# Attention probabilities scaled on ScalarE, the gate's Silu tied to a transpose copy, S5 products tied behind the mixing products

## The chip, the cores and the metric

The kernel runs on one core of a Trainium2 chip. The metric is the time of one execution on the device in microseconds (us). The engines are named as in the profile: PE is TensorE (matrix products and transposes), PEld its weight loads, DVE VectorE, ACT ScalarE, POOL GpSimd, SP SyncE, which issues most of the DMA transfers. PE's clock has two levels, 2.4 and 1.2 GHz; the profile's granted clock is 1.00 where the higher one was granted throughout.

## The reference

A decoder trunk of two layers over 1024 positions and 1024 channels, in float32. The change lies in the first layer's mixer, which has two groups of heads:

```
def rms_norm(x, g): y = x * rsqrt(mean(x * x) + EPS); return y * g
hn = rms_norm(x, norm_ab[i])
z = hn @ w_in_ab[i]
q, k, v, g_a, v_b, g_b = jnp.split(z, [...])           # 1024 columns each
a_out = dilated_attention(q, k, v) * jax.nn.silu(g_a)  # 16 heads of 64
b_out = multiscale_pool(v_b, pool_w[i], pool_scale[i]) * jax.nn.silu(g_b)
y = jnp.concatenate([a_out, b_out], axis=-1) @ w_out_ab[i]
```

`dilated_attention` mixes three causal patterns, (window, dilation) = (128, 1), (512, 4) and (2048, 16), by their softmax denominators, which is the same as one softmax over all keys of the three. In short: `p = exp(sc - m); o = (p / den) @ v`, with `den` the sum of a row of `p`.

The second layer has a gated spatial unit and an S5 state-space layer (complex diagonal states, 32 groups), whose tables depend on the parameters alone. After each mixer stands a cross-attention into 256 memory tokens.

## The kernel before

Large products are made in three passes (`mm3`, lines 199 to 207): weights and activations are split into a high part and a rest, and PE does high by high, high by rest, rest by high. The weights come through one planned queue: SP loads a tile of 128x1024 (`wst`), ACT rounds it to its high part (L177, `wh`), DVE subtracts (L178, `wl`).

The stage of the change is the input projection of the first layer, with the attention inside it. Two generators run against each other in `drive`: `ab_main` makes the projections, for each of 8 pairs of heads V (every second pair), then q, k and the gate `ga` (`ab_pair`, 24 products of 128x512 for each half of the sequence); after them the pooling group (`ab_pool`). `ab_side` does the attention. Each `yield 1` of `ab_main` (twice per 24 products) adds `rate` to an account, and at 1.0 one step of `ab_side` is written, so that a burst of attention stands after every 1 / `rate` yields. `yield 0` of the side means that it had nothing to do; `yield 2` of the main means that it waits for the side, and the next step is written at once.

One step of `ab_side` is one **burst**, for block b of 128 queries of a pair (8 blocks a pair, 64 in all):

- `turn` of the block before: PE transposes its probabilities `P` for two heads (L547, L551; PSUM tiles `ps_t`, two buffers), ACT copies the first part of each head to `PT` (L553), DVE copies the rest to `PTr` (L556).
- `front` of block b: PE's scores (L519, `ps_s`), then per head DVE's addition of the mask (L526) and maximum (L527), ACT's Exp with the row sum `den` (L528), DVE's reciprocal (L529) and multiplication of `P` by it (L530). A block has from 160 columns (b = 0) to 512 (b = 7).
- `mix` of the block before: PE's products of `PT` with V (L566, `ps_o`); after blocks 3 and 7 `last` (L577) adds the far keys and DVE multiplies by the gate (L580).

PE's instructions of this stage keep the written order (`in_order`); those of the other engines are placed by a scheduler, in which the side has the higher priority. Beside the bursts `behind` issues one step of `s5_prep`, the S5 tables, mostly small operations on POOL, some transposes and products on PE (L1125, L1131) and one reciprocal on DVE (L1028). These are `loose`: not held in PE's written order, but tied behind three instructions of the burst, `s.anchors`: the last score product, the last maximum and the last Exp.

In `ab_pair` the gate's Silu (L497) is issued when the second half of `ga` is evicted, and only then is the pair handed to the attention.

Of the kernel before, what the change touches and what calls it, by code (L numbers as in the profile page):

```python
# [95 lines left out]
class Prog:  # L96
# [372 lines left out]
    def ab_pair(s, pr):  # L469
        nc = s.nc  # L470
        q, kk, ga = (s.b(n) for n in ("q", "kk", "ga"))
        V, Vp = s.b("V"), s.b("Vp")
        vd, c0 = s.vd[pr // 2], 128 * (pr % 2)
        for r in range(4):
            nc.sync.dma_start(V[32 * r:32 * r + 32, :].rearrange("i (t c) -> i t c", t=8),
                              vd[:, c0:c0 + 128].rearrange("(t i r) c -> r i t c", i=32, r=4)[r])
        for hh in range(2):
            nc.sync.dma_start(Vp[:, 512 * hh:512 * hh + 512].rearrange("p (r c) -> p r c", r=4),
                                vd[512 * hh:512 * hh + 512, c0:c0 + 128].rearrange("(p r) c -> p r c", r=4))
        held, R8 = {}, s.R8  # L480
        for h in range(2):
            yield from s.proj(("ab", pr), h, held)
            s.anchor = nc.vector.tensor_tensor(q[:, 512 * h:512 * h + 512].rearrange("p (b r i) -> p b r i", b=4, r=4),
                                               s.last.rearrange("p (b i r) -> p b r i", b=4, r=4),
                                               R8[h].rearrange("p (b i r) -> p b r i", b=4, r=4), op=ALU.mult)
            yield 1
        for h in range(2):
            yield from s.proj(("ab", 8 + pr), h, held)
            s.anchor = nc.vector.tensor_tensor(kk[:, 512 * h:512 * h + 512].rearrange("p (b r i) -> p b r i", b=4, r=4),
                                               s.last.rearrange("p (b i r) -> p b r i", b=4, r=4),  # L490
                                               s.R[h].rearrange("p (b i r) -> p b r i", b=4, r=4), op=ALU.mult)
            yield 1
        for h in range(2):
            yield from s.proj(("ab", 16 + pr), h, held)
            s.anchor = nc.vector.tensor_tensor(ga[:, 512 * h:512 * h + 512], s.last, s.R[h], op=ALU.mult)
            if h == 1:
                nc.scalar.activation(ga, ga, AF.Silu)  # L497
            yield 1
        s.pair[pr] = (q, kk, ga, V, Vp)

    def attn(s, pr):

# [4 lines left out]
        def front(b):  # L507
# [15 lines left out]
            for e in range(2):  # L523
                t = s.u("P")
                mx, den = s.col("mx"), s.col("den")
                nc.vector.tensor_tensor(t[:, :n], p[e][:, :n], s.cst[:, m0:m0 + n], op=ALU.add)  # L526
                i = nc.vector.tensor_reduce(mx, t[:, :n], axis=AX.X, op=ALU.max, negate=True)  # L527
                j = nc.scalar.activation(t[:, :n], t[:, :n], AF.Exp, bias=mx, accum_out=den)  # L528
                nc.vector.reciprocal(den, den)  # L529
                nc.vector.tensor_scalar(t[:, :n], t[:, :n], den, None, op0=ALU.mult)  # L530
                P[b, e] = t
            s.anchors += [i, j]

        def turn(b):
# [8 lines left out]
            for e in range(2):  # L543
# [6 lines left out]
                    c0 = 128 * (nb + k)  # L550
                    nc.tensor.transpose(pt[:, c0:c0 + 128], t[:, 128 * k:128 * k + 128], s.ident)  # L551
                PT[b, e] = s.u("PT")
                nc.scalar.activation(PT[b, e][:, :n1], pt[:, :n1], AF.Copy)  # L553
                for k in range(kt):
                    w, c0 = min(128, n2 - 128 * k), 128 * (nb + k)
                    nc.vector.tensor_copy(PTr[half, e][:w, 512 * k:512 * k + 512].rearrange("p (r b i) -> p r b i", r=4, b=4)[:, :, b4, :],  # L556
                                          pt[:w, c0:c0 + 128].rearrange("p (r i) -> p r i", r=4))

        def mix(b):
            half, b4 = b // 4, b % 4  # L560
            nb = 1 if b == 0 else 2
            for j in range(nb):
                blk = b - nb + 1 + j
                for e in range(2):
                    ov = o[half][64 * e:64 * e + 64, :].rearrange("p (r b i) -> p r b i", r=4, b=4)[:, :, b4, :]
                    nc.tensor.matmul(ov, lhsT=V[:, 128 * blk + 64 * e:128 * blk + 64 * e + 64],  # L566
                                     rhs=PT[b, e][:, 128 * j:128 * j + 128].rearrange("p (r i) -> p r i", r=4),
                                     start=(b4 == 0 and j == 0), stop=False, skip_group_check=True)

# [25 lines left out]
    def ab_side(s):  # L595
# [3 lines left out]
        for n in range(64 + 2):  # L599
            pr, b = divmod(n, 8)  # L600
            if n < 64:
                while pr not in s.pair:
                    yield 0
                if b == 0:
                    made[pr] = s.attn(pr)
            was, wb = divmod(n - 1, 8)
            if 0 < n <= 64:
                made[was][1](wb)
            if n < 64:
# [38 lines left out]
    def ab_main(s):  # L648
        s.R8 = [s.u("R8") for _ in range(2)]
        for h in range(2):  # L650
            s.nc.gpsimd.tensor_scalar(s.R8[h], s.R[h], 0.125, None, op0=ALU.mult)
        s.vd, s.pair, s.gd, s.attn_done = {}, {}, {}, -1
        for pr in range(8):
            if pr % 2 == 0:
                yield from s.ab_v(pr // 2)
# [830 lines left out]
def build(nc, tc, a):  # L1486
    with tc.tile_pool(name="sb", bufs=1) as pool, tc.tile_pool(name="ps", bufs=1, space=MS.PSUM) as psum, \
# [11 lines left out]
        s.phase = "ab"  # L1499
        s.mtags = ("mm",)  # L1500
        mark = len(nc.cur_bb.bb.instructions)
        drive(tc, s.ab_main(), s.ab_side(), 0.55, -500)
        pe = [i for i in nc.cur_bb.bb.instructions[mark:] if i.engine == s.anchors[0].ins.engine]
        s.in_order(pe[0], pe[-1])
        s.mtags = wide
# [27 lines left out]
```

## Time and profile before

| | |
|---|---|
| time, median of 3 runs | 2112.68 us (2112.36 to 2113.53) |
| the profiled execution | 2116.89 us, span 2115.2 us |
| granted clock, mean over the span | 0.989 |
| PE busy | 2061.8 us (97%) |
| DVE busy | 1144.8 us (54%) |
| ACT busy | 767.5 us (36%) |
| POOL busy | 534.8 us (25%) |

The span is the time from the first to the last instruction on the core. Busy time counts what an engine executes, not its waits. The attention bursts lie between about 260 and 835 us of the span.

### The profile page before, as it was taken

To read this page: it belongs to the slowest core of one execution; us is meant where nothing else is said; L and a number is where in the kernel's file an instruction comes from. 1 tells how busy PE (TensorE), PEld (TensorE's weight loads), DVE (VectorE), ACT (ScalarE), POOL (GpSimd) and SP (SyncE) were. 2 spreads that over 40 slices of the span, in tenths; PEclk is the share of its full clock that TensorE was granted. 3 is DMA by queue.
4 is the path that set the end of the run, shared out by engine and by line. 5 is a ranking of instruction groups with operands and counts; after the bars stand their busy time and mean duration, and the time that the engine had idled before them with its cause. 6 is when DMAs were issued, how large, how long until landed. Compare 5 with 4: busy or idle time off the path is not lost.

```text
span 2115.2 us, 33157 instructions
## 1 busy us (share of the span) xinstructions
PE 2061.8 (97%) x12974; PEld 1729.7 (82%) x12974; DVE 1144.8 (54%) x2067; ACT 767.5 (36%) x1442; POOL 534.8 (25%) x802
## 2 busy tenths in 40 slices
PE   8999999899999988999999999999999999999998
PEld 8999888687787766888888888888888887888887
DVE  6664266566655775456453655444653334555554
ACT  7765243333333333114332444212221122443453
POOL 4332017722333244122111003221221100220013
PEclk9999999999999999999999999999999999999999
DMA  7888212103114112116464125532331134642142
GB/s 293 301 292 281 73 33 86 56 24 119 51 65 114 62 51 86 56 66 222 146 208 164 46 101 183 166 119 70 116 113 70 58 102 157 202 165 74 51 169 80
DMA packets 131468, 258.63 MB, mean 122 GB/s; under 512 B 13040, under 2 KB 63344, under 8 KB 131312
## 3 DMA queue, kind: packets, MB, share of 16 engines
q1 hardware_dynamic: 86608, 189.39, 26.8%
q0 software_dynamic: 13440, 43.53, 5.6%
q10 hardware_dynamic: 31264, 23.60, 3.6%
q8 instruction: 102, 1.67, 0.3%
q14 instruction: 54, 0.44, 0.1%
HBM read 193.02 MB, written 63.44 MB: 121 GB/s over the span
## 4 chain that ended last, share of the span: by engine, by line
PE 87%; DVE 5%; POOL 3%; ACT 2%; issue 2%; DMA 1%; SPq 0%; DVEq 0%; ACTq 0%; POOLq 0%
PE ps_mm L203 13%; PE ps_mm L204 13%; PE ps_mm L205 13%; PE ps_s L204 5%; PE ps_s L205 5%; PE ps_s L203 5%; PE ps_o L205 4%; PE ps_o L204 4%; PE ps_o L203 4%; PE ps_s L519 2%; PE ps_o L566 1%; PE ps_mm L1311 1%; PE ps_mm L1309 1%; PE ps_mm L1310 1%; PE ps_t L547 1%
## 5 line engine op out<-in xcount | busy, mean ns | idle before, releaser
L178 DVE TENSOR_TENSOR wl<-wst,wh 128x1024 fp32r<-128x1024 f32 (+1 forms) x263 | 345.8, 1329 | 128.3 <-ACT wh L177 123.3
L203 PE MATMUL ps_mm<-xg,wh 128*128 128x512 f32 x880 | 350.1, 398 | 1.3 <-DVE ug L1338 1.0
L204 PE MATMUL ps_mm<-xg,wh 128*128 128x512 f32 x880 | 343.7, 391 | 0.0
L205 PE MATMUL ps_mm<-xg,wl 128*128 128x512 f32 x880 | 343.3, 390 | 0.0
L177 ACT ACTIVATE wh<-wst 128x1024 fp32r<-128x1024 f32 (+1 forms) x263 | 262.0, 1016 | 113.4 <-PE ps_mm L204 84.5
L203 PEld LDWEIGHTS ps_mm<-xg,wh 128*128 128x128 f32 x880 | 165.4, 188 | 43.3 <-issue 8.3
L205 PEld LDWEIGHTS ps_mm<-xg,wl 128*128 128x128 f32 x880 | 165.3, 188 | 34.9
L204 PEld LDWEIGHTS ps_mm<-xg,wh 128*128 128x128 f32 x880 | 165.6, 188 | 32.4 <-issue 0.2
L240 POOL TENSOR_TENSOR acc<-acc,sq 128x512 f32<-128x512 f32 (+1 forms) x81 | 102.5, 1266 | 215.0 <-ACT sq L236 202.5
L223 ACT ACTIVATE xg<-x,gains 128x512 fp32r<-128x512 f32 x64 | 46.2, 722 | 246.3 <-DVE x L753 187.4
L528 ACT ACTIVATE P<-P,mx 128x320 f32<-128x320 f32 (+7 forms) x128 | 77.9, 610 | 136.6 <-DVE mx L527 132.9
L553 ACT ACTIVATE PT<-ps_t 128x256 f32<-128x256 f32 (+1 forms) x128 | 45.3, 369 | 174.2 <-PE ps_t L551 172.7
L592 POOL DMA_DIRECT2D gab<-G x32 | 18.1, 567 | 244.2 <-DVE G L580 126.9
L530 DVE TENSOR_SCALAR P<-P,den 128x320 f32<-128x320 f32 (+7 forms) x128 | 77.2, 604 | 4.4
L556 DVE COPY PTr<-ps_t 128x128 f32<-128x128 f32 (+2 forms) x192 | 46.0, 281 | 55.8 <-ACT PT L553 52.8
L224 DVE SCALAR_TENSOR_TENSOR xg<-x,gains,xg 128x512 fp32r<-128x512 f32 x64 | 52.1, 815 | 42.1 <-ACT xg L223 40.8
L203 PE MATMUL ps_mm<-wh,xg 128*128 128x256 f32 x256 | 73.9, 289 | 0.0
L205 PE MATMUL ps_mm<-wh,xg 128*128 128x256 f32 x256 | 72.5, 283 | 0.0
L204 PE MATMUL ps_mm<-wl,xg 128*128 128x256 f32 x256 | 72.4, 283 | 0.0
L1338 DVE TENSOR_TENSOR ug<-ps_mm,R 128x512 f32<-128x512 f32 x32 | 22.1, 689 | 90.4 <-PE ps_mm L205 90.3
L526 DVE TENSOR_TENSOR P<-ps_s,cst 128x320 f32<-128x320 f32 (+7 forms) x128 | 65.0, 549 | 8.3 <-PE ps_s L519 6.4
L547 PE MATMUL ps_t<-cst,P 128*128 128x128 f32 x240 | 47.5, 281 | 21.0 <-DVE den L529 15.0
(423 smaller groups left out, 5115.1 us busy)
## 6 DMA issues: line engine op xcount, KB each, us to landing
wst<-w_ab SPq DMA_DIRECT2D x40, 512.0 KB, 3.4
wst<-w_out_ab SPq DMA_DIRECT2D x32, 512.0 KB, 4.3
wst<-vsc SPq DMA_DIRECT2D x32, 512.0 KB, 4.0
wst<-w_kv SPq DMA_DIRECT2D x31, 512.0 KB, 5.9
wst<-w_cd SPq DMA_DIRECT2D x24, 512.0 KB, 3.4
wst<-w_out_cd SPq DMA_DIRECT2D x32, 384.0 KB, 3.3
wst<-w_q SPq DMA_DIRECT2D x16, 512.0 KB, 8.1
msc<-mo ACTq DMA_DIRECT2D x32, 256.0 KB, 6.2
```

What stands on the lines that cost most here:

```text
L177: s.last_hi = s.nc.scalar.activation(H[:, :w], t[:, :w], AF.Copy)
L178: s.nc.vector.tensor_tensor(L[:, :w], t[:, :w], H[:, :w], op=ALU.subtract)
L203: s.nc.tensor.matmul(ps, lhsT=lh, rhs=rh, start=(i == 0), stop=False)
L204: s.nc.tensor.matmul(ps, lhsT=lh, rhs=rl, start=False, stop=False)
L205: s.nc.tensor.matmul(ps, lhsT=ll, rhs=rh, start=False, stop=(i == n - 1))
L223: nc.scalar.activation(H, x, AF.Copy, scale=g)
L224: nc.vector.scalar_tensor_tensor(L, x, g, H, op0=ALU.mult, op1=ALU.subtract)
L240: nc.gpsimd.tensor_tensor(st["acc"][:, :n], st["acc"][:, :n], q[:, :n], op=ALU.add)
L526: nc.vector.tensor_tensor(t[:, :n], p[e][:, :n], s.cst[:, m0:m0 + n], op=ALU.add)
L528: j = nc.scalar.activation(t[:, :n], t[:, :n], AF.Exp, bias=mx, accum_out=den)
L530: nc.vector.tensor_scalar(t[:, :n], t[:, :n], den, None, op0=ALU.mult)
L547: nc.tensor.transpose(pt[:, 128 * j:128 * j + 128], t[:, n2 + 128 * j:n2 + 128 * j + 128], s.ident)
```

## The change

The multiplication of the probabilities by `1/den` goes from a DVE `tensor_scalar` to an ACT Copy with a per-row scale. A pair is handed to the attention before its gate is projected; the Silu of the gate is issued in the burst that turns block 2, tied behind the second PT copy, and `ab_side` waits there until the gate is projected. The first of the three anchors of the S5 steps is the last mixing product in place of the last score product. The rate of bursts goes from 0.55 to 0.52.

```diff
--- before.py
+++ after.py
@@ -490,13 +490,13 @@
                                                s.last.rearrange("p (b i r) -> p b r i", b=4, r=4),
                                                s.R[h].rearrange("p (b i r) -> p b r i", b=4, r=4), op=ALU.mult)
             yield 1
+        s.pair[pr] = (q, kk, ga, V, Vp)
         for h in range(2):
             yield from s.proj(("ab", 16 + pr), h, held)
             s.anchor = nc.vector.tensor_tensor(ga[:, 512 * h:512 * h + 512], s.last, s.R[h], op=ALU.mult)
             if h == 1:
-                nc.scalar.activation(ga, ga, AF.Silu)
+                s.gated.add(pr)
             yield 1
-        s.pair[pr] = (q, kk, ga, V, Vp)
 
     def attn(s, pr):
 
@@ -527,7 +527,7 @@
                 i = nc.vector.tensor_reduce(mx, t[:, :n], axis=AX.X, op=ALU.max, negate=True)
                 j = nc.scalar.activation(t[:, :n], t[:, :n], AF.Exp, bias=mx, accum_out=den)
                 nc.vector.reciprocal(den, den)
-                nc.vector.tensor_scalar(t[:, :n], t[:, :n], den, None, op0=ALU.mult)
+                nc.scalar.activation(t[:, :n], t[:, :n], AF.Copy, scale=den)
                 P[b, e] = t
             s.anchors += [i, j]
 
@@ -550,11 +550,14 @@
                     c0 = 128 * (nb + k)
                     nc.tensor.transpose(pt[:, c0:c0 + 128], t[:, 128 * k:128 * k + 128], s.ident)
                 PT[b, e] = s.u("PT")
-                nc.scalar.activation(PT[b, e][:, :n1], pt[:, :n1], AF.Copy)
+                i = nc.scalar.activation(PT[b, e][:, :n1], pt[:, :n1], AF.Copy)
                 for k in range(kt):
                     w, c0 = min(128, n2 - 128 * k), 128 * (nb + k)
                     nc.vector.tensor_copy(PTr[half, e][:w, 512 * k:512 * k + 512].rearrange("p (r b i) -> p r b i", r=4, b=4)[:, :, b4, :],
                                           pt[:w, c0:c0 + 128].rearrange("p (r i) -> p r i", r=4))
+            if b == 2:
+                with s.tc.issue_after(i.ins):
+                    nc.scalar.activation(ga, ga, AF.Silu)
 
         def mix(b):
             half, b4 = b // 4, b % 4
@@ -563,7 +566,7 @@
                 blk = b - nb + 1 + j
                 for e in range(2):
                     ov = o[half][64 * e:64 * e + 64, :].rearrange("p (r b i) -> p r b i", r=4, b=4)[:, :, b4, :]
-                    nc.tensor.matmul(ov, lhsT=V[:, 128 * blk + 64 * e:128 * blk + 64 * e + 64],
+                    s.anchors[0] = nc.tensor.matmul(ov, lhsT=V[:, 128 * blk + 64 * e:128 * blk + 64 * e + 64],
                                      rhs=PT[b, e][:, 128 * j:128 * j + 128].rearrange("p (r i) -> p r i", r=4),
                                      start=(b4 == 0 and j == 0), stop=False, skip_group_check=True)
 
@@ -604,6 +607,8 @@
                 if b == 0:
                     made[pr] = s.attn(pr)
             was, wb = divmod(n - 1, 8)
+            while wb == 2 and was not in s.gated:
+                yield 0
             if 0 < n <= 64:
                 made[was][1](wb)
             if n < 64:
@@ -649,7 +654,7 @@
         s.R8 = [s.u("R8") for _ in range(2)]
         for h in range(2):
             s.nc.gpsimd.tensor_scalar(s.R8[h], s.R[h], 0.125, None, op0=ALU.mult)
-        s.vd, s.pair, s.gd, s.attn_done = {}, {}, {}, -1
+        s.vd, s.pair, s.gated, s.gd, s.attn_done = {}, {}, set(), {}, -1
         for pr in range(8):
             if pr % 2 == 0:
                 yield from s.ab_v(pr // 2)
@@ -1499,7 +1504,7 @@
         s.phase = "ab"
         s.mtags = ("mm",)
         mark = len(nc.cur_bb.bb.instructions)
-        drive(tc, s.ab_main(), s.ab_side(), 0.55, -500)
+        drive(tc, s.ab_main(), s.ab_side(), 0.52, -500)
         pe = [i for i in nc.cur_bb.bb.instructions[mark:] if i.engine == s.anchors[0].ins.engine]
         s.in_order(pe[0], pe[-1])
         s.mtags = wide
```

What this does to the order of the instructions, at three places. First PE, where the third pair begins (block 0 of the pair; the bursts that turn block 7 of the pair before and then block 0). Before:

```order
L519 MATMUL ps_s<-kk,q 32x128 x8
L519 MATMUL ps_s<-kk,q 32x32 x8
L566 MATMUL ps_o<-PT,V 64x4x32 x4
L547 MATMUL ps_t<-cst,P 128x128
L551 MATMUL ps_t<-cst,P 128x128
L547 MATMUL ps_t<-cst,P 128x128
L551 MATMUL ps_t<-cst,P 128x128
L519 MATMUL ps_s<-kk,q 32x256 x8
L519 MATMUL ps_s<-kk,q 32x64 x8
L566 MATMUL ps_o<-PT,V 64x4x32 x2
```

After the change:

```order
L519 MATMUL ps_s<-kk,q 32x128 x8
L519 MATMUL ps_s<-kk,q 32x32 x8
L569 MATMUL ps_o<-PT,V 64x4x32 x4
L203 MATMUL ps_mm<-xg_648,wh 128x512
L204 MATMUL ps_mm<-xg_648,wh 128x512
L205 MATMUL ps_mm<-xg_648,wl 128x512
...
L547 MATMUL ps_t<-cst,P 128x128
L551 MATMUL ps_t<-cst,P 128x128
```

The mixing products (L566, now L569) were followed at once by the transposes of the next burst; now 24 products of the projection stand between (8 times the three rows shown).

ACT, at the gate of the third pair (`ga`); L528 is Exp, L553 the copy of transposed probabilities. Before:

```order
L528 ACTIVATE P,den<-P,mx 128x512 x2
L553 ACTIVATE PT<-ps_t 128x256
L497 ACT_TABLE_LOAD
L497 ACTIVATE ga<-ga 128x1024
L553 ACTIVATE PT<-ps_t 128x256
L528 ACT_TABLE_LOAD
L528 ACTIVATE P,den<-P,mx 128x160 x2
L553 ACTIVATE PT<-ps_t 128x128 x2
```

After the change:

```order
L553 ACTIVATE PT<-ps_t 128x256 x2
L560 ACT_TABLE_LOAD
L560 ACTIVATE ga<-ga 128x1024
L528 ACT_TABLE_LOAD
L528 ACTIVATE P,den<-P,mx 128x384 x2
L530 ACTIVATE P<-P,den 128x384 x2
```

The table load and the Silu stood between the two PT copies of a burst; now they stand behind both, with the load for Exp and the exponentials of the next block behind them, and the scaling (L530) follows the exponentials on ACT.

DVE, at the reciprocal of the S5 tables (L1028, now L1033; `s5z`), in the burst that turns block 7 of the second pair. Before:

```order
L495 TENSOR_TENSOR ga<-ps_mm,R_81 128x512
L556 COPY PTr<-ps_t 128x4x32 x2
L1028 RECIPROCAL s5z<-s5z 128x48
L526 TENSOR_TENSOR P<-ps_s,cst 128x160 x2
L527 TENSOR_REDUCE mx<-P 128x1
L556 COPY PTr<-ps_t 128x4x32 x2
L527 TENSOR_REDUCE mx<-P 128x1
L529 RECIPROCAL den<-den 128x1
L530 TENSOR_SCALAR P<-P,den 128x160
```

After the change:

```order
L529 RECIPROCAL den<-den 128x1
L489 TENSOR_TENSOR kk<-ps_mm,R_81 128x512
L529 RECIPROCAL den<-den 128x1
L1033 RECIPROCAL s5z<-s5z 128x48
L556 COPY PTr<-ps_t 128x4x32 x4
L526 TENSOR_TENSOR P<-ps_s,cst 128x160 x2
L527 TENSOR_REDUCE mx<-P 128x1 x2
L529 RECIPROCAL den<-den 128x1 x2
```

The reciprocal stands ahead of all copies of the burst and ahead of the next block's additions; the multiplications L530 are gone from the queue.

## Rows read from the trace of the kernel before

**Rows 1.** Attention stage: us; busy PE, PEld, DVE, ACT, POOL; clock; DMA share; GB/s.

```profile
280.00:840.00 560.00, 529.24 (x5047) 425.73 (x5046) 354.96 (x819) 200.54 (x462) 235.13 (x476) 0.97 0.21 67
```

**Rows 2.** PE's waits by releaser in 280 to 840 us: total, times, longest.

```profile
PE ps_t L547 <- DVE den L529: 15.0, 8, 5.7
PE ps_o L566 <- ACT PT L553: 9.2, 5, 2.2
PE ps_t L547 <- DVE P L530: 5.8, 6, 3.8
PE ps_t L1125 <- DVE PTr L556: 0.5, 1, 0.5
```

**Rows 3.** Timeline, all engines, 379 to 396 us: start, us, engine, line, operation [idle before].

```profile
379.61 1.29 DVE L526 TENSOR_TENSOR P<-ps_s,cst 128x512 f32<-128x512 f32 x2
...
383.95 0.48 DVE L530 TENSOR_SCALAR P<-P,den 128x512 f32<-128x512 f32 x1
...
384.24 0.19 ACT L528 ACTIVATION_READ_ACCUMULATOR P<-P,mx 128x1 f32 x1
...
385.61 0.38 PE L547 MATMUL ps_t<-cst,P 128*128 128x128 f32 x2
...
386.25 0.38 ACT L553 ACTIVATE PT<-ps_t 128x256 f32<-128x256 f32 x1 [1.82 <-PE ps_t L551]
...
386.65 1.28 ACT L497 ACT_TABLE_LOAD   x1
...
387.94 1.06 ACT L497 ACTIVATE ga<-ga 128x1024 f32<-128x1024 f32 x1
...
389.33 0.65 PE L566 MATMUL ps_o<-PT,V 128*64 128x128 f32 x6 [1.88 <-ACT PT L553]
...
392.01 0.45 DVE L1028 RECIPROCAL s5z<-s5z 128x48 f32<-128x48 f32 x1 [4.86 <-POOL s5z L909]
...
395.69 0.45 PE L547 MATMUL ps_t<-cst,P 128*128 128x128 f32 x1 [5.71 <-DVE den L529]
```

**Rows 4.** Timeline of PE: the first rows of two bursts, and of one's mixing.

```profile
539.24 0.45 PE L547 MATMUL ps_t<-cst,P 128*128 128x128 f32 x1 [1.81 <-DVE den L529]
...
685.00 0.30 PE L547 MATMUL ps_t<-cst,P 128*128 128x128 f32 x1 [1.81 <-DVE den L529]
...
828.22 0.67 PE L566 MATMUL ps_o<-PT,V 128*64 128x128 f32 x6 [2.21 <-ACT PT L553]
```

**Rows 5.** Two DVE lines, 280 to 840 us: durations in ns (min/median/max).

```profile
L530 DVE TENSOR_SCALAR P<-P,den x124: 302/436/6804, 279.8 to 824.2; 128x352 f32<-128x352 f32 x16, 128x384 f32<-128x384 f32 x16, 128x416 f32<-128x416 f32 x16, 128x448 f32<-128x448 f32 x16
L178 DVE TENSOR_TENSOR wl<-wst,wh x30: 846/1224/3406, 291.0 to 822.4; 128x1024 fp32r<-128x1024 f32 x29, 128x512 fp32r<-128x512 f32 x1
```

**Rows 6.** Timeline, the four long multiplications, one POOL product, one PE wait.

```profile
727.78 4.57 DVE L530 TENSOR_SCALAR P<-P,den 128x448 f32<-128x448 f32 x1
728.00 2.05 POOL L909 TENSOR_TENSOR s5co<-s5i,yz 128x1024 f32<-128x1024 f32 x1
...
744.29 6.80 DVE L530 TENSOR_SCALAR P<-P,den 128x512 f32<-128x512 f32 x1
...
751.24 0.66 PE L547 MATMUL ps_t<-cst,P 128*128 128x128 f32 x2 [3.79 <-DVE P L530]
...
790.84 2.18 DVE L530 TENSOR_SCALAR P<-P,den 128x416 f32<-128x416 f32 x1
...
812.09 3.52 DVE L530 TENSOR_SCALAR P<-P,den 128x480 f32<-128x480 f32 x1
```

**Rows 7.** Three stretches of 10 us (columns as in Rows 1).

```profile
390.00:400.00 10.00, 4.31 (x56) 3.32 (x58) 4.79 (x17) 3.34 (x10) 6.12 (x25) 0.59 0.00 0
540.00:550.00 10.00, 10.00 (x90) 8.06 (x89) 3.98 (x11) 1.69 (x6) 3.34 (x3) 0.73 0.08 28
...
750.00:760.00 10.00, 8.66 (x65) 6.74 (x66) 5.67 (x17) 3.93 (x8) 4.27 (x6) 0.66 0.01 2
```

**Rows 8.** One ACT group by shape, 280 to 840 us: count, busy, mean ns, idle before.

```profile
L528 ACT ACTIVATE P<-P,mx 128x512 f32<-128x512 f32 x16 | 11.4, 716 | 18.4 <-DVE mx L527 18.4
```

## Prediction

> **What bounds the kernel now.** I read the busy time by stage first. In the stage that the change touches, 280 to 840 us, PE is busy for 529.2 of 560 us: it stands still for 30.8, with a mean granted clock of 0.97 [rows 1]. Every other engine there is below two thirds, so PE is the bound, and only what makes PE wait, or lowers its clock, can be won. Then PE's waits in that stretch, by releaser: 15.0 us for `den` in front of the transposes L547, 5.8 for `P` at the same place, 9.2 for `PT` in front of the mixing products L566, 0.5 in front of the S5 transposes L1125; together 30.5 [rows 2]. So all of PE's idle time is named, and it all belongs to the attention bursts.
>
> Then the timeline, to see what is late in each kind of wait.
>
> *Silu in the middle.* At 386.25 ACT copies the first transposed block (0.38), then loads a table (1.28), does the gate's Silu (1.06), and only then copies the second block; L566 waits 1.88 [rows 3]. The three waits of 1.88 have this cause (389, 537, 683 us; one of them shown); the other two of the five, 1.34 and 2.21, come from the same thing done by the pooling gate's Silu near 807 and 828 us [rows 2, 4].
>
> *Bursts without products between.* At 389.3 the mixing of one burst is followed at once by the next burst's transposes, whose probabilities aren't made yet: 5.71 us of wait, of which DVE's S5 reciprocal L1028, which waits 4.86 for POOL at the head of DVE's queue, is the larger part [rows 3]. The same gap stands at 539 and 685 us without L1028, 1.81 each [rows 4]. These three are 9.3 of the 15.0.
>
> *The multiplication by `den`.* L530 takes 0.436 at the median and 6.804 at most [rows 5]. The long ones (4.57, 6.80, 2.18, 3.52) lie where POOL runs S5 products without a pause, as beside the product of 2.05 at 728 us; behind the longest PE waits 3.79 [rows 6]. The remaining five `den` waits (5.6) and this 3.79 make 9.4; nearly all of it is these four.
>
> *The clock.* It falls only after such idle time: 0.59 in 390 to 400 us, 0.73 in 540 to 550, 0.66 in 750 to 760 [rows 7], that is from 2.4 to 1.2 GHz for part of each. Busy time times shortfall is 1.8 + 2.7 + 2.9 = 7.4 us; with smaller falls elsewhere I take 10, of which 1 belongs to the pooling gate.
>
> **The change, part by part.**
>
> *Earlier pairs, rate 0.52.* In the changed order no burst follows another without products. The three empty gaps hold 24 products now; before, eight more gaps held only 12 products of 512 columns or 24 of 256, after it two do, and five hold about 4 us of products. Gain: 9.3 of waiting. What comes back: the reciprocal (L1033 now) still stands ahead of the next block's work in DVE's queue, and POOL's steps are as long as before. POOL finished it at 392.0, 6.4 us after the burst's first transposes at 385.61 [rows 3]. From there the changed chain needs four copies, two additions, two maxima, two exponentials and a multiplication on 160 columns, about 4.4 us by the durations of these rows' kinds, so P comes 10.8 after the burst's start, and PE, with 24 products to do, arrives after 7.5. I count 3.3 of wait and 1 of clock (bounds 0, if POOL gains from the multiplications that no longer hold it up, and 5.7, the wait of before).
>
> *Silu behind the second copy.* It gives back the three times 1.88, 5.6. What is queued behind it on ACT are the next block's exponentials: table, Silu, table are 3.6 us from the end of the second copy, and that block's first maximum is ready after about 2 (two additions take 1.29 at the widest [rows 3], a maximum about half of that), so P comes some 1.5 later in eight bursts. The cover is the 24 products; a gap with three quarters of their time (two of the eight bursts) leaves up to 0.8. The pooling gate's Silu isn't moved: in the changed order it still stands between two copies, twice, and its 3.5 us of wait stay.
>
> *Scaling on ACT.* DVE loses 128 multiplications (two a block, 64 blocks), ACT gains them. The trace of this stage has no Copy on ACT with a per-row scale from SBUF to SBUF at these widths; the nearest row is the Exp on 128x512, which has a per-row operand too, 0.716 [rows 8], and DVE's own median for all widths, 0.436 [rows 5], bounds it below. I take 0.72 at the widest; the changed order has no table load for it. In the order ACT does both exponentials and then both copies, so in the burst at 380 us, a slow one with a weight split among its additions, the first scaled block would be ready at 384.43 + 0.72 = 385.15 rather than 384.43, and PE came for it at 385.61 [rows 3]. So even there 0.7 more is hidden by the 24 products; this is the widest block. In the seven short or middle gaps I count 0 to 0.8 each, 2.7 in all, and 3 for the pooling stretch, where ACT rounds pooled values between exponentials. Won: the 9.4.
>
> The Trainium skill, "SBUF — State Buffer", section "Who interferes with whom", says that a `tensor_scalar` between SBUF operands can take the port pair that DVE shares with GpSimd, and then waits for the whole instruction of the other, while ACT waits for no one. The trace agrees: median 0.436, longest 6.804 beside a busy POOL [rows 5, 6]. "ScalarE: Activation LUTs", section "Rules for kernel authors", speaks against the change: multiply on VectorE. By medians the trace agrees (0.436 against 0.72); by that rule each block costs 0.3 more, and the sum would lose its 9.4.
>
> *S5 products behind the mixing.* L1125 no longer stands among the L566 rows: 0.5, and their four transposes lie between bursts; the same work, nothing else.
>
> Sum: 9.3 + 5.6 + 9.4 + 0.5 + 9 of clock = 33.8 won; 4.3 + 2.7 + 3 given back, less 1.7 of small waits in today's short gaps, which are `P` waits beside the 3.79: 8.3. Net 25.5. The profiled execution has a span of 2115.2 and took 2116.9, 4.2 over the median of 2112.7; taken off that median the forecast is **2087 us**.
>
> **The rivals.**
>
> *The lock moves.* With L530 gone, the splits L178 are what DVE runs beside POOL from SBUF; one took 3.406 [rows 5], and they stand between maxima and reciprocals. (The same section of the skill says that an operation with two SBUF inputs contends with a GpSimd that reads.) 30 splits, median 1.22: if three of them cost a wait like the 2 us now seen, 6 us come back: 2093.
>
> *A thin gain.* L1033 costs its full 5.7 and a fall of the clock, and the short gaps and the pooling stretch twice what I count: 2087 + 3.4 + 5.7 = 2096; with only half of the clock won back 2101.
>
> *The change does nothing to speak of*: POOL's lateness, not DVE's lock, sets P, and waits move from one name to another: 2112. Against it: the gaps of 1.81 have no POOL in them.
>
> *Slower: ACT becomes the chain.* ACT is busy 200.5 of 560 [rows 1] and gets some 75 more (128 copies at about 0.6). If P came later by more than the products hide, at all 64 bursts, every 0.7 of lateness would cost 45 and eat the 33.8: +11, 2124. It decides from a mean spare time below 0.2 us; the widest block still had 0.46 left above.
>
> **Numbers.** Chances: forecast 0.62, the lock moves 0.12, thin gain 0.18, nothing 0.03, slower 0.05. The most that can be won is all idle time and clock, 40.5 (2072). The forecast's own bounds are 33.8 won with nothing given back, 2079, and what is given back doubled, 2095. For 8 in 10 I reach from 2076 to 2102. A measurement here tells about 0.2%, 4.2 us: faster 0.92, same 0.03, slower 0.05.
>
> **What would show it.** Right: no wait of 1.8 for `PT` outside the pooling gate; no L547 wait above 1 us outside the burst of L1033 and the pooling stretch; the ACT copy near 0.72 with no outlier where POOL is full; clock 1.00 in nearly all of 400 to 780 us; PE idle in the stage near 10. Wrong: L547 waits for ACT at most bursts (the slower rival), long L178 just ahead of waits (the lock moved), a fall of the clock after L1033.

## The result, and the profile after

The changed kernel takes 2084.61 us (median of 4 runs, 2084.09 to 2086.72); the kernel before, beside it, 2113.11 (4 runs, 2112.36 to 2114.3). The ratio is 0.9866, with a 95% interval of 0.9849 to 0.9884: 28.5 us faster, where 25.5 was forecast. The profiled execution took 2084.09, its span is 2082.1.

The stage of [rows 1], in the changed kernel (same columns):

```profile
280.00:840.00 560.00, 547.44 (x5145) 445.12 (x5130) 296.42 (x709) 266.70 (x582) 238.36 (x484) 0.99 0.22 72
```

PE stands still for 12.6 us instead of 30.8. The waits that answer to [rows 2]:

```profile
PE ps_t L547 <- ACT P L530: 6.9, 5, 2.5
PE ps_o L569 <- ACT PT L553: 3.5, 2, 2.1
PE ps_t L547 <- DVE PTr L556: 0.8, 1, 0.8
PE ps_mm L203 <- DVE q L483: 0.7, 1, 0.7
PE ps_t L547 <- ACT s5wz L1131: 0.4, 1, 0.4
```

The 15.0 for `den` are gone. The 9.2 for `PT` are 3.5, and 6.9 are new for `P`, which ACT makes now. PE's timeline says where these two names stand:

```profile
740.52 0.44 PE L547 MATMUL ps_t<-cst,P 128*128 128x128 f32 x2 [1.09 <-ACT P L530]
742.97 0.44 PE L547 MATMUL ps_t<-cst,P 128*128 128x128 f32 x2 [1.90 <-ACT P L530]
760.83 0.44 PE L547 MATMUL ps_t<-cst,P 128*128 128x128 f32 x2 [0.92 <-ACT P L530]
773.64 0.65 PE L569 MATMUL ps_o<-PT,V 128*64 128x128 f32 x6 [1.34 <-ACT PT L553]
790.58 0.44 PE L547 MATMUL ps_t<-cst,P 128*128 128x128 f32 x2 [2.47 <-ACT P L530]
794.35 0.90 PE L569 MATMUL ps_o<-PT,V 128*64 128x128 f32 x5 [2.14 <-ACT PT L553]
```

Together with one of 0.56 at 343 us they make up both lines. So nearly all of it lies between 740 and 795 us, where the pooling projections run under the last attention blocks; in what follows this is the pooling stretch. Windows of 10 us (columns as in [rows 1]) show the clock's part; the first answers to [rows 7]:

```profile
390.00:400.00 10.00, 10.00 (x82) 7.97 (x81) 4.55 (x11) 3.87 (x9) 7.21 (x29) 1.00 0.24 80
...
740.00:750.00 10.00, 7.58 (x62) 5.58 (x63) 5.03 (x11) 7.76 (x13) 0.72 (x2) 0.83 0.00 0
...
790.00:800.00 10.00, 7.28 (x28) 5.21 (x28) 2.36 (x7) 4.14 (x6) 0.58 (x1) 0.66 0.14 52
```

The two places where it still falls are the two with the longest waits. Over the whole span PE is busy for 2045.6 us instead of 2061.8, with the same 12974 instructions: 16.2 less for the same work. About 11 of it is the mean granted clock, by an estimate from the two profiles (0.989 of 2115.2 us, 0.994 of 2082.1); the rest isn't placed.

The two DVE lines of [rows 5]; the first is on ACT now:

```profile
L530 ACT ACTIVATE P<-P,den x120: 412/627/727, 284.4 to 790.4; 128x416 f32<-128x416 f32 x16, 128x448 f32<-128x448 f32 x16, 128x480 f32<-128x480 f32 x16, 128x512 f32<-128x512 f32 x16
L178 DVE TENSOR_TENSOR wl<-wst,wh x34: 849/1225/3222, 280.0 to 838.3; 128x1024 fp32r<-128x1024 f32 x32, 128x512 fp32r<-128x512 f32 x2
```

The longest scaling takes 0.727, where 6.804 stood. One weight split L178 still takes 3.222, and it is the start of the longest wait for `P`:

```profile
780.61 3.22 DVE L178 TENSOR_TENSOR wl<-wst,wh 128x1024 fp32r<-128x1024 f32 x1
...
783.86 0.33 SPq L159 DMA_DIRECT2D wst<-w_ab  x1
...
787.38 1.06 ACT L177 ACTIVATE wh<-wst 128x1024 fp32r<-128x1024 f32 x1 [6.12 <-DMA wst<-w_ab]
```

The split runs beside POOL's S5 products, which end at 782.74. SP issues the next transfer into the staging tile 0.03 us after the split's end. ACT's rounding L177, which stands ahead of the next block's exponentials, waits for that transfer; then come the exponentials, the scaling, and PE's wait of 2.47 at 790.58.

### The profile page after: what moved, and what is told of

Its sections match the earlier page's. It is cut to its first block, busy times and chain, and to the rows that moved or that the text cites. A ratio compares the mean times of both kernels' runs of the same rounds, so it can differ in the third digit from the quotient of the medians.

```text
span 2082.1 us, 33021 instructions
## 1 busy us (share of the span) xinstructions
PE 2045.6 (98%) x12974; PEld 1719.0 (83%) x12974; DVE 1070.1 (51%) x1939; ACT 834.1 (40%) x1570; POOL 529.3 (25%) x802
## 4 chain that ended last, share of the span: by engine, by line
PE 59%; DVE 2%; issue 0%; ACT 0%; POOL 0%; DVEq 0%
PE ps_mm L203 7%; PE ps_mm L204 7%; PE ps_mm L205 7%; PE ps_s L204 4%; PE ps_s L205 4%; PE ps_s L203 4%; PE ps_o L204 3%; PE ps_o L205 3%; PE ps_o L203 3%; PE ps_mm L1316 1%; PE ps_mm L1314 1%; PE ps_mm L1315 1%; PE ps_o L819 1%; PE ps_o L818 1%; PE ps_o L820 1%; PE ps_s L818 1%
## 5 line engine op out<-in xcount | busy, mean ns | idle before, releaser
L178 DVE TENSOR_TENSOR wl<-wst,wh 128x1024 fp32r<-128x1024 f32 (+1 forms) x263 | 345.3, 1327 | 144.2 <-ACT wh L177 141.2
L177 ACT ACTIVATE wh<-wst 128x1024 fp32r<-128x1024 f32 (+1 forms) x263 | 262.2, 1016 | 109.8 <-PE ps_mm L204 83.5
L205 PEld LDWEIGHTS ps_mm<-xg,wl 128*128 128x128 f32 x880 | 165.5, 188 | 34.9
L528 ACT ACTIVATE P<-P,mx 128x320 f32<-128x320 f32 (+7 forms) x128 | 78.0, 610 | 150.3 <-DVE mx L527 150.2
L553 ACT ACTIVATE PT<-ps_t 128x256 f32<-128x256 f32 (+1 forms) x128 | 45.7, 370 | 112.8 <-PE ps_t L551 110.2
L595 POOL DMA_DIRECT2D gab<-G x32 | 18.2, 569 | 222.7 <-DVE G L583 96.3
L530 ACT ACTIVATE P<-P,den 128x320 f32<-128x320 f32 (+7 forms) x128 | 72.7, 604 | 5.3 <-DVE den L529 5.3
L204 PE MATMUL ps_s<-gr,wh 128*128 128x512 f32 x168 | 65.8, 392 | 2.1 <-DVE gr L211 2.1
```

The lines of the kernel that those rows point to most:

```text
L177: s.last_hi = s.nc.scalar.activation(H[:, :w], t[:, :w], AF.Copy)
L178: s.nc.vector.tensor_tensor(L[:, :w], t[:, :w], H[:, :w], op=ALU.subtract)
L204: s.nc.tensor.matmul(ps, lhsT=lh, rhs=rl, start=False, stop=False)
L205: s.nc.tensor.matmul(ps, lhsT=ll, rhs=rh, start=False, stop=(i == n - 1))
L530: nc.scalar.activation(t[:, :n], t[:, :n], AF.Copy, scale=den)
```

## The experiments

My theory was that of the prediction: the parts of the change have worths of their own, which add (in the expectations: **parts**). The rival: what counts is only that no burst stands directly behind another, and then neither the Silu nor the place of the scaling matters (**spacing**). Twelve kernels ran in three groups, each beside runs of the kernel before on its own chip, so every difference is taken to the kernel before of its own group. Where two kernels are compared below, it is by these differences. In kernels whose edits add lines the line numbers are shifted by a few (L530 is L531, GpSimd's L914 is L922).

| kernel | median us (runs) | before there | difference | ratio, 95% interval |
|---|---|---|---|---|
| changed | 2084.61 (4) | 2113.11 | -28.5 | 0.9849 to 0.9884 |
| l_dve_scale: changed, scaling on DVE | 2086.01 (4) | 2115.11 | -29.1 | 0.9852 to 0.9879 |
| l_silu_gate: changed, Silu at the gate | 2090.30 (4) | 2115.11 | -24.8 | 0.9874 to 0.9904 |
| l_anchor: changed, old S5 tie | 2087.86 (4) | 2114.30 | -26.4 | 0.9857 to 0.9886 |
| l_rate55: changed, rate 0.55 | 2079.42 (4) | 2114.30 | -34.9 | 0.9819 to 0.9848 |
| l_dve55: both of these | 2094.73 (4) | 2115.08 | -20.4 | 0.9885 to 0.9918 |
| o_early: before, early pairs | 2101.77 (5) | 2115.11 | -13.3 | 0.9928 to 0.9953 |
| o_act_scale: before, scaling on ACT | 2109.95 (11) | 2115.11 | -5.2 | 0.9969 to 0.9990 |
| o_rate52: before, rate 0.52 | 2130.32 (4) | 2115.08 | +15.2 | 1.0053 to 1.0086 |
| v_gate: changed, pooling Silu tied | 2083.84 (4) | 2114.30 | -30.5 | 0.9829 to 0.9863 |
| v_gate_round: and the rounding | 2077.24 (4) | 2114.30 | -37.1 | 0.9807 to 0.9836 |
| v_nolock: and the last S5 products | 2072.31 (4) | 2115.08 | -42.8 | 0.9779 to 0.9808 |
| v_all55: all three, rate 0.55 | 2079.87 (4) | 2115.08 | -35.2 | 0.9809 to 0.9845 |

**One part taken back.** Scaling on DVE again:

```diff
-                nc.scalar.activation(t[:, :n], t[:, :n], AF.Copy, scale=den)
+                nc.vector.tensor_scalar(t[:, :n], t[:, :n], den, None, op0=ALU.mult)
```

> The changed kernel with one part undone: the multiplication by 1/den is on DVE again; order of the bursts, Silu and anchors stay as changed. The parts theory (each part is worth what its waits were): long multiplications of 2 to 7 us return beside POOL's S5 products, PE waits behind them for about 9 us with a fall of the clock, so 2084.6 + 9 = about 2094 us, and the S5 reciprocal, which POOL then makes late again, may add 3. The spacing theory (once 24 products stand between all bursts, everything else is hidden): the long multiplications are there but PE hardly waits, 2085 to 2087 us.

The time is that of the changed kernel, as spacing had it; parts missed by some 8 us. PE's waits in this run, 265 to 870 us:

```profile
PE ps_t L547 <- DVE P L530: 5.4, 3, 3.2
PE ps_o L569 <- ACT PT L553: 4.6, 3, 2.2
PE ps_t L547 <- DVE den L529: 4.2, 2, 3.6
```

The 5.4 and 4.2 look like the 9.4 that the prediction gave to the locked multiplications, but the timeline says otherwise (ACT, DVE and PE):

```profile
739.06 1.14 ACT L210 ACTIVATE plr<-pl 128x512 fp32r<-128x512 f32 x2
...
744.67 0.41 PE L547 MATMUL ps_t<-cst,P 128*128 128x128 f32 x2 [3.24 <-DVE P L530]
...
780.50 5.22 DVE L530 TENSOR_SCALAR P<-P,den 128x480 f32<-128x480 f32 x1
...
785.87 0.41 PE L547 MATMUL ps_t<-cst,P 128*128 128x128 f32 x2 [3.59 <-DVE den L529]
```

Only the 3.59 stands behind a locked multiplication, of 5.22. The 3.24, and a wait of 1.72 at 763.73, stand where the changed kernel waits 1.09 + 1.90 and 0.92: there ACT rounds pooled values (L210) between the two exponentials of a block, whichever engine scales, and the multiplications take 0.39 to 0.77. And the split that took 3.22 in the changed kernel takes 1.22 in this one. So POOL's run of S5 products meets a multiplication in this run and a split in the changed kernel, and the time is the same. The same run bears on the S5 reciprocal L1033. First it, then its counterpart in the changed kernel, whose burst begins at 377.04 (377.00 with the scaling on DVE):

```profile
381.11 0.45 DVE L1033 RECIPROCAL s5z<-s5z 128x48 f32<-128x48 f32 x1 [4.78 <-POOL s5z L914]
```

```profile
377.04 0.38 PE L547 MATMUL ps_t<-cst,P 128*128 128x128 f32 x2
...
378.81 0.45 DVE L1033 RECIPROCAL s5z<-s5z 128x48 f32<-128x48 f32 x1 [3.14 <-POOL s5z L914]
```

At this one place POOL comes to the reciprocal 2.3 us earlier with DVE's multiplications gone.

The Silu issued at the gate's eviction again, with the early pairs kept:

```diff
             if h == 1:
+                nc.scalar.activation(ga, ga, AF.Silu)
                 s.gated.add(pr)
...
-            if b == 2:
-                with s.tc.issue_after(i.ins):
-                    nc.scalar.activation(ga, ga, AF.Silu)
```

> The changed kernel with one part undone: the gate's Silu is issued when the gate is evicted, not tied behind a transpose copy; the pair is still handed over early. In the order of this kernel it stands between the two copies of a burst once (second pair) and between the two scalings of a block twice; elsewhere it falls between bursts. The parts theory: one wait near 1.9 us and two near 1, so 2 to 5 us over the changed kernel, 2087 to 2090 us. The spacing theory: the early pairs alone moved it out of the way, at most 2 us over, 2085 to 2086.5 us.

Slower by 3.7, which fits parts, though the intervals overlap. Waits, 265 to 870 us: 15.5 in all, against 12.3 in the changed kernel.

```profile
PE ps_t L548 <- ACT P L531: 9.2, 8, 2.4
PE ps_o L567 <- ACT PT L554: 4.3, 3, 1.6
```

Only one `PT` wait more than in the changed kernel, not three as in the kernel before: in the changed spacing the gate's eviction mostly doesn't fall between two copies any more.

The old tie of the S5 products (`s.anchors[0]` stays the last score product):

> The changed kernel with the tie of the loose S5 products set back to the last score product. Both theories expect little: the trace of before has only 0.5 us of TensorE waits at an S5 transpose. Theory parts, with its 10 us for this and the spacing number: if the tie has the larger share of them, 2088 or more; if the spacing number has them, 2084 to 2085.5.

2.1 above, within the interval: no difference that these runs can tell.

**One part alone.** The pairs handed early in the kernel before (with the attention's wait for the gate at block 2, not shown), and the scaling alone:

```diff
+        s.pair[pr] = (q, kk, ga, V, Vp)
         for h in range(2):
             yield from s.proj(("ab", 16 + pr), h, held)
...
-        s.pair[pr] = (q, kk, ga, V, Vp)
```

> The kernel before with one part done: the pair is handed over before its gate (and the attention waits at block 2 for the gate); rate 0.55, scaling on DVE, Silu at the gate and anchors as before. No two bursts follow each other without products now, six gaps hold 12 products. The parts theory: the three empty gaps give back 9.3 us of waits and about 5 of clock, two of the three Silu waits stay, the long multiplications stay: 2113 - 14 = about 2099 us. The spacing theory: nearly the whole gain, 2087 to 2092 us.

> The kernel before with one part done: the multiplication by 1/den on ACT; everything else as before, so the three empty gaps and eight short ones stay. The parts theory: the waits behind the long multiplications (9.4 us with some clock, 12) go, and the longer chain costs about 0.5 in each of the eleven empty or short gaps, so 2113 - 12 + 5.5 = about 2106 us. The spacing theory: the lock's waits move to other causes and the longer chain costs, 2111 to 2118 us.

The early pairs alone are worth 13.3, the 14 of parts; the three empty places go. The scaling alone is worth 5.2, where parts took off 6.5 and spacing at most 2. Their waits of PE, 265 to 870 us, o_early first:

```profile
PE ps_t L548 <- DVE P L531: 17.4, 10, 8.9
PE ps_t L548 <- DVE den L530: 3.8, 3, 2.6
```

```profile
PE ps_t L547 <- ACT P L530: 19.7, 14, 3.0
PE ps_o L566 <- ACT PT L553: 8.9, 5, 2.0
```

Take one cause away and most of the wait turns up under the next name: PE's idle time in this stretch is 30.8 before, 26.7 and 28.8 here. Up to here some 10 us of the 28.5 were on no part, so I gave them to the rate and took that back:

```diff
-        drive(tc, s.ab_main(), s.ab_side(), 0.52, -500)
+        drive(tc, s.ab_main(), s.ab_side(), 0.55, -500)
```

> The changed kernel with one number set back: the attention blocks advance by 0.55 per step again instead of 0.52, everything else as changed. Theory parts (each part has its own worth; the changed kernel stands 17.2 us below the kernel that only hands the pairs early, of which the Silu has 5.7 and the scaling 1.4, so some 10 are left for the spacing number and the anchor): 2090 to 2096, with TensorE waits for the scaled probabilities in bursts that stand only 12 products behind the burst before. Theory spacing (once the pairs are handed early no burst stands directly behind another, and the rest of the spacing does not matter): 2084 to 2086.5.

Both missed: 6.4 us **faster** than the changed kernel. The table of stages (columns as in [rows 1]), changed kernel first, then this one:

```profile
265.00:735.00 470.00, 467.31 (x4644) 382.43 (x4645) 250.01 (x626) 235.43 (x527) 200.48 (x415) 1.00 0.22 71
735.00:865.00 130.00, 120.13 (x730) 95.25 (x729) 61.91 (x112) 44.23 (x76) 40.24 (x74) 0.96 0.20 69
```

```profile
265.00:735.00 470.00, 464.33 (x4624) 379.20 (x4623) 248.68 (x621) 235.58 (x527) 195.16 (x409) 1.00 0.22 69
735.00:865.00 130.00, 126.60 (x811) 100.87 (x810) 68.86 (x122) 44.63 (x78) 48.70 (x83) 1.00 0.24 80
```

The rate of 0.52 does what it was credited with up to 735 us (2.7 of idle against 5.7) and loses more in the pooling stretch (9.9 against 3.4, and the clock). So I tried it with the scaling on DVE, and alone on the kernel before:

> The changed kernel with the spacing number at 0.55 and the scaling back on VectorE. Theory spacing (with the pairs early no burst stands so close that the locked multiplication or the longer ScalarE chain decides; where the scaling runs is worth 2 us at most): 2077.5 to 2081.5. Theory closeness (at 0.55 some bursts stand 12 products apart, and there a locked multiplication is a wait of 3 to 6 us on TensorE): 2086 to 2092.

> The kernel before with the spacing number at 0.52 alone. The three places where a burst stands directly behind the one before it stay, since the pairs are still handed late, and the Silu and the locked multiplications stay. Theory parts of the prediction (the number and the early pairs remove the empty places together): 2105 to 2110. Theory early pairs alone (the number only moves which block meets what): 2110 to 2117.

With the scaling on DVE the step from 0.52 to 0.55 costs 8.7 instead of giving 6.4, a little more than closeness had it; the step the other way, to 0.52, makes the kernel before 15.2 slower, where the higher of the two expectations ended at 2117. One event is the largest piece of the first, here on DVE, POOL and PE:

```profile
778.41 11.99 DVE L530 TENSOR_SCALAR P<-P,den 128x480 f32<-128x480 f32 x1
```

```profile
788.88 1.26 POOL L914 TENSOR_TENSOR Ei<-s5w,s5w 128x512 f32<-128x512 f32 x1
```

```profile
790.55 0.66 PE L547 MATMUL ps_t<-cst,P 128*128 128x128 f32 x2 [8.88 <-DVE P L530]
```

A multiplication of 0.44 stands from 778.41 to 790.40, to the end of POOL's run of S5 products at 790.14; PE waits 8.88 for it. o_early, at 0.55 with the scaling on DVE too, has a wait of 8.9 as well. In the kernel before at 0.52 an addition of the pooling window (1.23 undisturbed) meets that run, whose last products end at 778.57, and then PE waits:

```profile
771.05 8.60 DVE L679 TENSOR_TENSOR win<-vb 128x1023 f32<-128x1023 f32 x1
```

```profile
776.53 2.04 POOL L909 TENSOR_TENSOR s5w<-Ei,trig 128x512 f32<-128x512 f32 x2
```

```profile
784.08 0.66 PE L547 MATMUL ps_t<-cst,P 128*128 128x128 f32 x2 [4.99 <-DVE P L530]
```

So what weighs most here isn't closeness, as I had expected it, but what DVE happens to issue during POOL's longest run, and the rate shifts that. I called this theory **phase**. These runs show it for the longest waits; the other waits of the two kernels haven't been traced one by one.

**The pooling stretch mended.** First the pooling gates' Silu behind both copies of the next block, as the change does for `ga`:

```diff
-            if b == 2:
-                with s.tc.issue_after(i.ins):
+            with s.tc.issue_after(i.ins):
+                if b == 2:
                     nc.scalar.activation(ga, ga, AF.Silu)
+                for g in s.pend:
+                    nc.scalar.activation(g, g, AF.Silu)
+            s.pend.clear()
...
+                if h == 1:
+                    s.pend.append(gb[d2])
...
-            nc.scalar.activation(gb[d2], gb[d2], AF.Silu)
...
+            if any(g is gb[d2] for g in s.pend):
+                s.pend = [g for g in s.pend if g is not gb[d2]]
+                nc.scalar.activation(gb[d2], gb[d2], AF.Silu)
```

> The changed kernel with the pooling gates' Silu also issued behind both transposed copies of the next block (two of them, the ones that still fall between blocks). Theory waits (what is left in the pooling stretch are waits of TensorE on ScalarE's queue): the waits for the transposed copy, 3.5 us in two pieces, go, and with the second of them part of a fall of the clock: 2079 to 2082. Theory return (a Silu put behind the copies makes the next exponentials late and the time comes back there): 2084 to 2086.

No difference that can be told. The 3.5 of `PT` waits are gone, but the `P` wait of 2.47 has grown to 4.29, and ahead of it stands a weight split:

```profile
782.34 5.05 DVE L178 TENSOR_TENSOR wl<-wst,wh 128x1024 fp32r<-128x1024 f32 x1
```

It is the split that took 3.22 in the changed kernel. So 1.8 of the 3.5 came back, as theory return had it, though by another way than a late exponential behind the Silu. Next the pooled values' rounding tied behind the newest block's second scaling (`s.scaled`):

```diff
-                s.hilo(t[:, :512], t[:, 512:], pl[:, 512 * h:512 * h + 512], nc.gpsimd)
+                with s.tc.issue_after(s.scaled.ins):
+                    s.hilo(t[:, :512], t[:, 512:], pl[:, 512 * h:512 * h + 512], nc.gpsimd)
```

> As the kernel before it, and the rounding of the pooled values on ScalarE tied behind the second scaling of the newest block, so that it no longer stands between the two exponentials of a block. Theory waits: of the 6.4 us of waits for the scaled probabilities in the pooling stretch the 3.9 at 740.5, 743.0 and 760.8 us go, and most of the fall of the clock to 0.83 there: 2074 to 2078. Theory return: as the kernel before it, within 1 us, because the scaling is late for another reason (the maximum on VectorE, or the weight rounding that follows).

6.6 better (the intervals just overlap), inside theory waits: the waits at 740.5, 743.0 and 760.8 are gone. One of 4.50 is left. Its rows, on DVE, POOL, SP, ACT and PE:

```profile
776.32 5.42 DVE L178 TENSOR_TENSOR wl<-wst,wh 128x1024 fp32r<-128x1024 f32 x1
```

```profile
778.61 2.05 POOL L922 TENSOR_TENSOR s5w<-Ei,trig 128x512 f32<-128x512 f32 x2
```

```profile
781.76 0.33 SPq L159 DMA_DIRECT2D wst<-w_ab  x1
```

```profile
785.12 1.06 ACT L177 ACTIVATE wh<-wst 128x1024 fp32r<-128x1024 f32 x1 [8.16 <-DMA wst<-w_ab]
```

```profile
788.32 0.69 PE L547 MATMUL ps_t<-cst,P 128*128 128x128 f32 x2 [4.50 <-ACT P L530]
```

To tell whether the split or the transfer behind it is at fault, the last S5 step, six products of 128x512, is queued behind the last attention output's store (`s.put`), so that POOL is nearly idle there:

```diff
+                while o8 == 1 and lv == 6 and s.attn_done < 7:
+                    yield 1
...
+                with s.tc.issue_after(s.put.ins) if o8 == 1 and lv == 6 else contextlib.nullcontext():
```

> As the kernel with gate and rounding tied, and the last and largest step of the S5 work on GpSimd (six products of 128x512, four of them between 776.6 and 780.6 us) queued behind the last attention output's store, so that GpSimd is idle when VectorE splits a weight (L178) between two blocks. Theory lock (that split took 5.42 us where 1.23 is its median, because GpSimd was in those products; it makes the next block's maxima late and frees the weight's staging tile late, so that the exponentials come late too): the split takes 1.2 to 1.3 us, the wait of 4.50 us of TensorE at 788.3 us falls below 1, and some 0.5 to 1 of clock comes with it: 2071.5 to 2074. Theory DMA (the exponentials stand behind a weight rounding that waits for its transfer, and the transfer is late for its own reasons): the split is short, the wait stays above 3, 2076 to 2078.

```profile
774.86 1.39 DVE L178 TENSOR_TENSOR wl<-wst,wh 128x1024 fp32r<-128x1024 f32 x1
```

```profile
776.28 0.33 SPq L159 DMA_DIRECT2D wst<-w_ab  x1
```

```profile
779.84 1.06 ACT L177 ACTIVATE wh<-wst 128x1024 fp32r<-128x1024 f32 x1 [4.34 <-DMA wst<-w_ab]
```

```profile
783.04 0.44 PE L547 MATMUL ps_t<-cst,P 128*128 128x128 f32 x2 [0.68 <-ACT P L530]
```

Theory lock, nearly with its numbers: the split is back at 1.39, the rounding that waits for the transfer into the staging tile starts 4.98 us after the split's start instead of 8.80, the wait is 0.68, the time 2072.31. The transfer itself is not what was late: both times SP issues it 0.02 or 0.03 us after the split's end, and the rounding starts 3.36 us later in the one run, 3.56 in the other. Against the kernel ahead of it the gain is 5.7, with intervals that just touch; all four runs here lie below all four there (2072.74 at most against 2074.20 at least). This is the best kernel of the study, below the changed one as well: -42.8 against -28.5, intervals apart. PE's whole idle time in the pooling stretch is now 1.2 us, at full clock:

```profile
735.00:865.00 130.00, 128.84 (x788) 103.78 (x787) 70.24 (x126) 46.11 (x79) 46.59 (x81) 1.00 0.24 81
```

Last, the same three ties at 0.55:

> The same three ties with the spacing number at 0.55. Theory phase (what the spacing number changes in the pooling stretch is which blocks meet the gates and the S5 work there; with the three ties that no longer matters, and what is left is the attention stretch, where 0.55 has 5.5 us of TensorE waits and 0.52 has 2.5): 2074 to 2077, slower than its twin at 0.52 by 1 to 4. Theory fewer blocks (0.55 is better in the pooling stretch because fewer blocks are left for it, whatever they meet): 2069 to 2073, at or below its twin.

Both missed; it is level with 0.55 without the ties (-35.2 against -34.9). The `PT` waits and the long split that they were made for aren't there at 0.55, and they give one thing back: the tied Silu now delays the exponentials of a block with only 12 products in front of it (PE waits 1.73 for that block, 0.64 without the tie). The Silu stands between the second copy and the exponentials, which start at 783.56:

```profile
781.18 1.06 ACT L562 ACTIVATE gb<-gb 128x1024 f32<-128x1024 f32 x1
```

Another wait, at 636 us and touched by no tie, is 2.88 in this run and 1.34 without the ties; that one I haven't explained. Between 265 and 870 us PE waits 10.8 us in it, against 4.8 in its twin at 0.52. The two profiled executions lie 12.4 apart, the medians 7.6, so the waits are only part of it; the rest I haven't placed.

## Why the prediction was right, and where its steps were not

The time and the sign held, and the waits were sized well in sum: idle time in the stage fell by 18.2, where the terms without the clock make 24.8 won less 7.3 given back, 17.5. What is left of the 28.5, 10.3, stands against 8 forecast for the clock (the trace of before is of an execution 3.8 above this median, so the split between the two is good to about that). But the terms did not hold one by one, and that their errors cancel is in part luck: the rate costs 6.4 where a gain was counted, the scaling brings next to nothing at this rate, and the 4.3 given back for the reciprocal never had to be paid.

The runs give a whole path from the kernel before to the changed one, by differences: early pairs 13.3; with the tied Silu and the S5 tie 20.4; with the scaling on ACT 34.9; and with the rate at 0.52 back to 28.5. Taken the other way round from 20.4, the rate comes first and gives 8.7 (29.1), and the scaling then nothing (28.5). So rate and scaling are together worth 8.1, and neither has a worth of its own: from l_dve55, with the scaling on DVE at 0.55, each of the two takes away the wait of 8.88.

*Early pairs and rate.* The 9.3 of empty places are gone, and early pairs alone show 13.3, of which only 4.1 is idle time in 265 to 870 us: 9.3 went and other waits grew, so the larger part isn't in these waits (the mean granted clock rose from 0.989 to 0.992). Putting the rate into the same term was wrong: it saves 3.0 of idle time before 735 us and costs 6.5 after it. The step counted products between bursts and did not ask what the pooling stretch would meet.

*The reciprocal.* 3.3 and 1 were set down as given back; PE did not wait at all. The bound of 0 was the case. Of the reason named for it half is shown, at this one place: POOL has the reciprocal 1.8 us after the burst's start instead of 6.4 [rows 3], and 2.3 of these 4.6 are the multiplications that left DVE. But with them on DVE, 4.1 after the start, there was no such wait either, so the chain behind it was counted too long as well.

*The Silu.* 5.6 of waits are gone; taking it back at the changed spacing shows 3.2 of waits and 3.7 of time.

*Scaling on ACT.* The instruction was sized rightly (714 ns on average at 128x512, no outlier). The error is that 9.4 was set down as the worth of the four locked multiplications in whatever order the rest stands: with the scaling on DVE again in the changed order only 3.6 of wait stands behind a lock (l_dve_scale). In the pooling stretch 6.4 of waits for `P` are left, where 3 was allowed: 3.9 behind the rounding of pooled values, which stand there on either engine and go when the rounding is moved (v_gate_round), and 2.5 behind the split. The whole is worth nothing at 0.52 and 14.5 at 0.55 (-34.9 against -20.4).

*The pooling gate's Silu* kept its 3.5 exactly (1.34 and 2.14).

*The rivals.* The lock did move to L178, at one place: behind the split of 3.22 stand the wait of 2.47 and, with the `PT` wait of 2.14 that follows, the lowest clock of the stage, 0.66. That is one such wait where the rival had three, so the time stayed at the forecast; but the 5.7 of v_nolock shows that the mechanism has its price. ACT did not become the chain; a change without effect and the thin gain did not come.

*What would show it.* No `PT` wait outside the pooling gate, no L547 wait above 1 us before 740, clock 1.00 from 280 to 740: all seen. After 740 the clock falls, once within the 400 to 780 that the prediction named (0.83 in 740 to 750). A long L178 just ahead of a wait, a sign of the rival, was seen too. PE's idle time was 12.6 instead of near 10.

*The most that can be won* was put at 40.5, and v_nolock is 42.8 below the kernel before with 5.1 of idle time left. The clock's 10 in it was too small: 0.97 over the 529 us that PE is busy in [rows 1] is about 16 (an estimate from that row).

## What to carry to other kernels

Where two engines lock each other out, look for the longest unbroken run of the one and ask which instruction of the other will be issued inside it: moving that run to where nobody waits was worth 5.7 us here at the rate at which moving 128 multiplications to another engine was worth nothing, though that move was worth 14.5 at the other rate. The name of a wait is only its last link: the changed kernel and l_dve_scale show the same wait for `P` behind the rounding of pooled values, under the name of whichever engine scales. A rate that sets which block meets what should be read stage by stage, since it can win in one and lose in the next; and a change made of several parts is to be taken apart by leaving each out, since parts that won alone (5.2) may win nothing in the whole.

## What the hardware showed

One blocked DVE instruction waited through a whole run of GpSimd instructions, not only through the one in progress: 11.99 us for 0.44 of work, until 0.26 after the run's last product ended; 5.42 for a split that takes 1.39 in v_nolock, where POOL's products end 0.30 after its start. All five of these operations with two inputs (1.39, 3.22, 5.05, 5.42 and 8.60) ended 1.08 or 1.09 after the run's last product, nearly the 1.23 that such an operation takes undisturbed. It isn't always DVE that waits: earlier in the same chain of l_dve55, among products of 128x8 and 128x16, two multiplications took their usual 0.43 and 0.45 and a split 1.26, and it is POOL's pair of products that is stretched, to 1.36 where the next pair takes 0.39:

```profile
772.75 1.26 DVE L178 TENSOR_TENSOR wl<-wst,wh 128x1024 fp32r<-128x1024 f32 x1
772.90 1.36 POOL L914 TENSOR_TENSOR s5w<-Er,trig 128x16 f32<-128x16 f32 x2
```

Not only the multiplication with one operand tile is hit, but also `tensor_tensor` with both inputs in SBUF (5.42, and 8.60 for the window's addition). The Trainium skill, "SBUF — State Buffer", section "Who interferes with whom", says of such a `tensor_tensor` that it contends with a GpSimd instruction that reads SBUF, and the trace agrees; of the side that waits it says that it is blocked for the whole instruction of the other, and here the measurement goes further, to the end of a run of them.
